# A planner with per-engine hand-over delays, TensorE's side work held back a set time behind its operands, and the residual multiplied by the norm's factor on VectorE instead of GpSimd

## The chip, the cores and the metric

One core of one Trainium2 chip runs the whole program. The metric is the time of one execution in device microseconds, the median of several runs. The engines are named as the profile names them: PE is TensorE's matrix multiply and PEld its weight load, DVE is VectorE, ACT is ScalarE, POOL is GpSimd, SP is SyncE, which here only starts transfers.

## The reference

Two layers, each with a mixer of three branches and a feed-forward block with a short convolution, over 272 positions (16 learned ones and 256 of the sequence) and 1024 features, in float32. The reference pads to 384 and masks; the rows that count are these 272.

```python
for li in range(DEPTH):
    h = h + mixer(rms_norm(h, norm_mix_g[li]), w_in[li], w_branch[li], w_out[li], ...)
    h = h + conv_ffn(rms_norm(h, norm_ffn_g[li]), w_ffn_in[li], ffn_conv_w[li], ...)
h = rms_norm(h, norm_final_g)

def mixer(hn, ...):
    rq, rk, rv, rg, hq, hf, hi, hg, dq, dk, dv, mg = jnp.split(hn @ w_in, offs, axis=-1)
    branches = [retention(rq, rk, rv, rg), hgrn2(hq, hf, hi, hg), diff_attention(dq, dk, dv)]
    y_b = jnp.einsum('blnc,ncd->blnd', branches, w_branch)
    return jnp.sum(jax.nn.sigmoid(mg) * y_b, axis=2) @ w_out

def conv_ffn(hn, ...):
    c = conv_b + sum(conv_w[j] * shifted(hn @ w_ffn_in, j) for j in range(3))
    gate, val = jnp.split(c, 2, axis=-1)
    return (silu(gate) * val) @ w_ffn_out
```

`rms_norm` divides each row by the root of its mean square and multiplies by a gain per feature. In `diff_attention` each head makes two softmaxes of scores and takes one minus lambda times the other.

## The kernel before

**Layout.** Features lie on the 128 partitions, positions run along the free dimension, so `h` is 8 tiles of 128x272 and every weight matrix is cut into 128x128 tiles. To keep float32 accuracy at the fast matmul rate, each weight tile and each activation tile is split into a rounded part and a rest (`whi`, `wlo`, `xh`, `xl`), and a product is three matmuls, lines 915 to 917: `xh` with `whi`, `xl` with `whi`, `xh` with `wlo`. These are the **main** products; 9,432 of the 10,594 matmuls in the program belong to them. In layer 1 most of them are 258 columns wide instead of 272. All other PE work (scores, transposes, sums over partitions, small products of the branches) is called **side work** here, and one unbroken run of it between main products a side block.

**Weights.** They come in chunks of 8 tiles (128x1024) through three buffers. For each chunk SP starts a transfer to `wraw`, ACT copies it to `whi` and DVE subtracts to give `wlo` (class `_Weights`, line 612). Each of `whi` and `wlo` has four buffers.

**Pairs.** The main products run in a fixed sequence, `ORDER`, of named pairs of output tiles, for instance `hq 0` or `fi 3`; `fi` are the 22 pairs of the feed-forward's first matrix. Each pair takes 8 tiles deep times 2, that is 48 main matmuls.

**The norm's factor.** At the start of the `w_in` products and of the `fi` products the factor `rstd` is not known yet. The first four pairs (`DEFER = 4`) therefore use `h` times the gain alone, and their results are multiplied by `rstd` when they leave PSUM (for `fi` into `two_a`). When the fifth pair begins, `Norm.next` (line 862) makes `y = h * rstd` for the eight tiles, and from `y` a new `xh` (ACT) and `xl` (DVE); from then on nothing has to be multiplied afterwards. This text calls the place a **fold**. There are four of them: before the fifth pair of `w_in` and of `fi` in both layers. Before the change POOL makes `y`, one 128x272 product after another.

After a `fi` pair, ACT and DVE do the convolution: ACT scales the last tap into `two_b`, DVE adds the other two taps with four SCALAR_TENSOR_TENSOR instructions, ACT applies SiLU, DVE multiplies gate and value (`two_b`), ACT and DVE split the result into `ghi` and `glo`.

**Attention heads.** A head group of `diff_attention` starts with the scores of the 16 learned positions of four heads at once: PE writes `ds`, DVE and ACT make the softmax in `wts`, and PE transposes it (`wt`). Then come the four heads, each: scores `ds` on PE, masked copies with row sums `two_a` and `two_b` on DVE, exponentials on ACT, the difference of the two softmaxes into `two_a` on DVE, three transposes `wt` on PE (line 1317), two products `do`, and a norm over partitions (`hsq` on ACT, `hr` on POOL). There are two such groups in each layer. Meanwhile DVE also rotates the next queries and keys: a shuffle into `two_c`, two multiplications and an addition into `dq` or `dk`.

**The order.** No line of the program says when side work runs. Every instruction is recorded with an engine, a cost in microseconds, a due time (`key`) and its dependencies. `_Plan.order` (line 454) then plays all engines in time and picks for each engine the instruction that can start first, and among those the one with the lowest rank, which is the due time with corrections. For PE's side work the correction is `HOLD` (later) or, next to other side work whose operands have been there for `SURE`, `PULL` (earlier). A result is taken to be usable on another engine `CROSS = 0.4` us after its end. The engines then execute their lists in that order, each list strictly in sequence, and wait on semaphores. `behind` records one step of a branch and chains it to earlier steps of the same branch.

Of the kernel before, what the change touches and what calls it, by code (L numbers as in the profile page):

```python
# [48 lines left out]
BACK = 0.09  # L49
# [299 lines left out]
class _Op:  # L349
    __slots__ = ("engine", "run", "cost", "key", "func", "tiles", "need", "after", "ready", "fed")  # L350

    def __init__(self, engine, run, cost, key, func):
        self.engine, self.run, self.cost, self.key, self.func = engine, run, cost, key, func
        self.tiles, self.need, self.after, self.ready, self.fed = set(), 0, [], 0.0, 0.0


class _Plan:
# [3 lines left out]
    CROSS = 0.4  # L361
    FREE = 0.5
# [64 lines left out]
    def queue(self, first, last):  # L427

        first.need += 1
        last.after.append(first)  # L430
# [23 lines left out]
    def order(self):  # L454
# [49 lines left out]
        while len(out) < todo:  # L504
# [35 lines left out]
            if e == "pe":  # L540
                if op in mains:
                    cost += BACK if beside else 0.0
# [31 lines left out]
class _Engine:  # L574
# [5 lines left out]
    def __getattr__(self, method):  # L580
        f = getattr(self.engine, method)

        def call(*args, **kw):
# [7 lines left out]
            elif self.name == "pool" and method != "memset":  # L591
                cost += 1.6e-3 * n
            if method == "partition_all_reduce":
                cost = 0.4 + 5.4e-3 * n
# [6 lines left out]
            elif method == "matmul" and args[1].dtype == F32R:  # L601
                cost = max(0.107, n / 2400 + 0.003)
            elif method == "matmul":
                cost = max(0.214 if args[1].shape[-1] > 32 else 0.07, 4 * n / 2400)
            elif method == "dma_start":
                cost = self.fixed + self.each * n * outs[0].shape[0]
# [60 lines left out]
def _trace(ctx, tc, plan, a, depth, probe):  # L667
    nc = tc.nc
    act = _Engine(plan, nc.scalar, "act", 0.094, 0.833e-3)
    dve = _Engine(plan, nc.vector, "dve", 0.068, 1.042e-3)  # L670
# [148 lines left out]
    class Norm:  # L819
# [42 lines left out]
        def next(self):  # L862
# [29 lines left out]
    def products(xs, name, j, t0=0):  # L892
# [12 lines left out]
        cost = 3 * ((T - t0) / 2400 + 0.003)  # L905
# [724 lines left out]
```

## Time and profile before

| what | value |
|---|---|
| median of 3 runs | 1301.27 us (1298.95 to 1302.18) |
| the profiled execution | 1298.69 us |
| its span, first to last instruction | 1296.9 us |
| DVE busy in the span | 74% |
| ACT busy in the span | 65% |
| POOL busy in the span | 13% |
| granted TensorE clock | 0.999 |

The page's first part gives busy time by engine; matmuls overlap in it, so a busy PE does not by itself mean that no time is lost. Lost time on PE shows better in the waits of PEld, the weight load: it stands in front of each matmul and waits for the same operands. Many rows carry line 607, because that one line issues every recorded instruction that is not a main product; there the tile names tell the rows apart.

### The profile page before, as it was taken

Reading aid. Unit: us, or ns where it says so; the run is one execution under the profiler, and the core shown is the slowest. Engines: PE = TensorE matmul, PEld = TensorE weight load, DVE = VectorE, ACT = ScalarE, POOL = GpSimd, SP = SyncE. Lnnn points to the kernel's source line nnn. Section 1 sums busy time; section 2 is a strip of 40 time slices with the busy share of each in tenths; the row PEclk is TensorE's granted clock in tenths of the full one; section 3 lists DMA queues with packets and bytes.
Section 4 is the critical chain, followed back from the end, with each engine's and each line's share of the span. In section 5 each row is a group of like instructions: output and inputs, shape, how many; then the busy total and the mean of one; then the engine's idle time right before and its main releaser. Section 6 shows DMA issues by size and latency. Waiting matters only on the chain.

```text
span 1296.9 us, 28609 instructions
## 1 busy us (share of the span) xinstructions
PE 1284.4 (99%) x11678; PEld 1255.9 (97%) x11678; DVE 960.9 (74%) x1589; ACT 838.6 (65%) x1376; POOL 166.8 (13%) x204
## 2 busy tenths in 40 slices
PE   9999999999999999999999999999999999999998
PEld 9999999999999999999999999999999999999986
DVE  7675787698585789886575767786985867898843
ACT  6766585856676567666457664858567765777643
POOL 4001111222121020000030011112220310200000
PEclk9999999999999999999999999999999999999999
DMA  7654574543644545555555645745546456366653
GB/s 269 205 164 160 170 205 142 160 161 125 201 145 155 183 154 178 181 178 179 179 172 186 192 151 172 214 140 170 170 131 198 145 169 204 134 210 195 203 189 112
DMA packets 86868, 225.36 MB, mean 174 GB/s; under 512 B 32976, under 2 KB 33104, under 8 KB 86736
## 3 DMA queue, kind: packets, MB, share of 16 engines
q1 hardware_dynamic: 86448, 223.00, 54.3%
q8 instruction: 92, 1.51, 0.5%
q10 hardware_dynamic: 288, 0.52, 0.1%
q14 instruction: 40, 0.33, 0.1%
HBM read 216.16 MB, written 1.05 MB: 167 GB/s over the span
## 4 chain that ended last, share of the span: by engine, by line
PE 91%; DVE 6%; issue 1%; ACT 1%; DMA 0%; SPq 0%; DVEq 0%
PE main L915 27%; PE main L917 26%; PE main L916 26%; PE fo L1430 2%; PE fo L1431 2%; PE fo L1429 2%; DVE wlo L607 1%; PE lev L1107 1%; DVE two_b L607 1%; DVE two_a L607 1%; PE ds L1291 1%; PE ro L607 1%; PE ho L607 1%; PE do L607 1%; DVE two_c L607 1%
## 5 line engine op out<-in xcount | busy, mean ns | idle before, releaser
L915 PE MATMUL main<-xh,whi 128*128 128x272 f32 (+1 forms) x2368 | 682.0, 288 | 0.0
L916 PE MATMUL main<-xl,whi 128*128 128x272 f32 (+1 forms) x2368 | 672.8, 284 | 1.5 <-DVE xl L607 1.5
L917 PE MATMUL main<-xh,wlo 128*128 128x272 f32 (+1 forms) x2368 | 673.3, 284 | 0.8 <-DVE wlo L607 0.5
L607 DVE TENSOR_TENSOR wlo<-wraw,whi 128x1024 fp32r<-128x1024 f32 (+1 forms) x411 | 502.7, 1229 | 192.2 <-ACT whi L607 185.5
L607 ACT ACTIVATE whi<-wraw 128x1024 fp32r<-128x1024 f32 (+1 forms) x411 | 426.5, 1041 | 229.6 <-PE main L916 145.7
L917 PEld LDWEIGHTS main<-xh,wlo 128*128 128x128 f32 x2368 | 445.9, 188 | 2.5 <-DVE wlo L607 2.4
L916 PEld LDWEIGHTS main<-xl,whi 128*128 128x128 f32 x2368 | 446.1, 188 | 2.2 <-DVE xl L607 1.9
L915 PEld LDWEIGHTS main<-xh,whi 128*128 128x128 f32 x2368 | 446.2, 188 | 1.4 <-ACT whi L607 0.2
L607 DVE SCALAR_TENSOR_TENSOR two_b<-main,small,two_b 128x256 f32<-128x256 f32 (+2 forms) x144 | 65.3, 487 | 25.0 <-ACT two_b L607 23.3
L607 POOL PARTITION_ALL_REDUCE hr<-hsq x36 | 67.2, 1877 | 114.7 <-ACT hsq L607 112.5
L607 POOL TENSOR_TENSOR y<-h,rstd 128x272 f32<-128x272 f32 x32 | 34.5, 1111 | 318.1 <-ACT rstd L607 318.1
L607 ACT ACTIVATE two_b<-main,small 128x272 f32<-128x272 f32 (+1 forms) x72 | 37.3, 566 | 25.1 <-PE main L917 24.0
L915 PE MATMUL main<-ghi,whi 128*128 128x272 f32 x176 | 51.0, 290 | 0.0
L916 PE MATMUL main<-glo,whi 128*128 128x272 f32 x176 | 50.6, 287 | 0.0
L917 PE MATMUL main<-ghi,wlo 128*128 128x272 f32 x176 | 50.3, 286 | 0.0
L607 POOL COPY tails<-vsrc 128x32 f32<-128x32 f32 x32 | 10.6, 344 | 224.4 <-ACT vsrc L607 223.0
L915 PE MATMUL main<-b0hi,whi 128*128 128x272 f32 (+1 forms) x128 | 37.9, 296 | 0.0
L915 PE MATMUL main<-b1hi,whi 128*128 128x272 f32 (+1 forms) x128 | 37.9, 296 | 0.0
L915 PE MATMUL main<-yhi,whi 128*128 128x272 f32 (+1 forms) x128 | 36.4, 284 | 0.0
L916 PE MATMUL main<-b0lo,whi 128*128 128x272 f32 (+1 forms) x128 | 36.4, 284 | 0.0
L917 PE MATMUL main<-yhi,wlo 128*128 128x272 f32 (+1 forms) x128 | 36.4, 284 | 0.0
L916 PE MATMUL main<-b1lo,whi 128*128 128x272 f32 (+1 forms) x128 | 36.3, 284 | 0.0
(235 smaller groups left out, 1938.6 us busy)
## 6 DMA issues: line engine op xcount, KB each, us to landing
wraw<-in_w SPq DMA_DIRECT2D x402, 512.0 KB, 3.5
h<-in_h SPq DMA_DIRECT2D x4, 272.0 KB, 5.7
dec<-in_dec SPq DMA_DIRECT2D x2, 544.0 KB, 6.9
wraw<-in_w SPq DMA_DIRECT2D x4, 256.0 KB, 4.6
const<-in_const SPq DMA_DIRECT2D x1, 937.0 KB, 7.6
turned<-apart SPq DMA_TRANSPOSE x48, 3.0
gain<-in_gl SPq DMA_DIRECT2D x1, 512.0 KB, 5.2
out<-y ACTq DMA_DIRECT2D x2, 256.0 KB, 2.8
```

The source lines that it names most:

```text
L607: self.plan.add(self.name, lambda: f(*args, **kw), cost, outs, ins, args[2] if method == "activation" else None)
L915: nc.tensor.matmul(o, wh, hi, start=first, stop=False)
L916: nc.tensor.matmul(o, wh, lo, start=False, stop=False)
L917: nc.tensor.matmul(o, wl, hi, start=False, stop=last)
L1107: nc.tensor.matmul(o, keys, x, start=True, stop=True)
L1291: nc.tensor.matmul(ss[m][:, at : at + nk], q[half, hd, q0 : q0 + P], k[half, hd, :nk], start=True, stop=True)
L1429: nc.tensor.matmul(o, gh, wh, start=False, stop=False)
L1430: nc.tensor.matmul(o, gl, wh, start=False, stop=False)
L1431: nc.tensor.matmul(o, gh, wl, start=False, stop=end)
```

## The change

1. `y = h * rstd` at the four folds moves from POOL to DVE. POOL made eight 128x272 products per fold; DVE makes two of 128x1088. The due times move from 12 us ahead of the fifth pair (0.3 us apart) to 9 us ahead (2.8 us apart).
2. The planner's hand-over times change. `CROSS = 0.4` becomes a table by producing engine, `LAG` (0.12 to 0.20 us, 2.0 us for transfers); a dependent instruction on the same engine gets a delay of its own (`SAME`); a buffer is free again `LAG + 0.05` after its last use instead of 0.5. Links that only set a sequence (`queue`) carry no delay any more.
3. Side work on PE is held back until 0.7 us after its last operand from another engine (`SAFE`). The 0.09 us that each return from side work to main products cost in the plan (`BACK`) is dropped.
4. The costs of many instructions are changed in the plan. A main product of three matmuls of 272 columns is planned with 0.3685 us instead of 0.349.
5. A step of a head of `diff_attention` may begin when the step two before it has reached its eighth last instruction, instead of its last.

```diff
-BACK = 0.09
+SAFE = 0.7
...
-    CROSS = 0.4
-    FREE = 0.5
+    LAG = {"pe": 0.20, "act": 0.13, "dve": 0.12, "pool": 0.15, "sp": 2.0}
+    SAME = {"pe": 0.0, "act": 0.13, "dve": 0.12, "pool": 0.1, "sp": 0.0}
+    FREE = 0.05
...
         first.need += 1
-        last.after.append(first)
+        last.then.append(first)
...
             if op.engine == "pe" and op not in mains:
+                if op.fed + SAFE > t:
+                    return math.inf
                 return op.key - PULL if beside and op.fed + SURE <= t else op.key + HOLD
...
             if e == "pe":
-                if op in mains:
-                    cost += BACK if beside else 0.0
                 beside = op not in mains
...
-            done = t + cost + (2.0 if e == "sp" else 0.0)
+            done = t + cost
...
-                    free[self.tag[n]].append(done + self.FREE)
+                    free[self.tag[n]].append(done + self.LAG[e] + self.FREE)
...
                 if o.engine != e:
-                    o.fed = max(o.fed, done + self.CROSS)
-                o.ready = max(o.ready, done + (self.CROSS if o.engine != e else 0.0))
+                    o.fed = max(o.fed, done + self.LAG[e])
+                o.ready = max(o.ready, done + (self.LAG if o.engine != e else self.SAME)[e])
+                if o.need == 0:
+                    push(o)
+            for o in op.then:
+                o.need -= 1
+                o.ready = max(o.ready, done)
...
-            elif method == "matmul" and args[1].dtype == F32R:
-                cost = max(0.107, n / 2400 + 0.003)
             elif method == "matmul":
-                cost = max(0.214 if args[1].shape[-1] > 32 else 0.07, 4 * n / 2400)
+                cost = max(0.218 if args[1].shape[-1] > 32 else 0.07, 4 * n / 2400 + 0.02)
...
-    act = _Engine(plan, nc.scalar, "act", 0.094, 0.833e-3)
-    dve = _Engine(plan, nc.vector, "dve", 0.068, 1.042e-3)
+    act = _Engine(plan, nc.scalar, "act", 0.105, 0.833e-3)
+    dve = _Engine(plan, nc.vector, "dve", 0.065, 1.052e-3)
...
-                plan.key = clock[0] - 12.0 + 0.3 * k
                 if k % 4 == 0:
+                    plan.key = clock[0] - 9.0 + 0.7 * k
                     ys.append(slot4("y"))
+                    tt(ys[-1], h[:, k : k + 4, :], pair(rstd, 4), MUL)
                 y = ys[-1][:, k % 4, :]
-                pool.tensor_tensor(out=y, in0=h[:, k, :], in1=rstd, op=MUL)
                 plan.key = clock[0] - 6.0 + 0.7 * k
...
-        cost = 3 * ((T - t0) / 2400 + 0.003)
+        cost = 3 * ((T - t0) / 2400 + 0.0095)
...
-        def behind(f, until, apart=1):
+        def behind(f, until, apart=1, after=1):
...
-            mine.append(ops)
+            mine.append((ops, after))
             if len(mine) > apart:
-                plan.queue(ops[0], mine[-1 - apart][-1])
+                before, which = mine[-1 - apart]
+                plan.queue(ops[0], before[-which])
...
-                    behind(lambda: da_head(b, hd), "da", 2)
+                    behind(lambda: da_head(b, hd), "da", 2, 8)
```

The instructions themselves stay the same but for `y`: 32 fewer on POOL, 8 more on DVE. Besides, POOL's list has 4 bare ISA rows without operands instead of 7, and ACT's list has 33 loads of function tables instead of 29. PE's list has the same 10,594 matmuls; its side work stands in 123 blocks instead of 129. Three places show what moves.

First, DVE in layer 0, where the softmax of the learned positions (`wts`) is made for the transpose `wt` that PE waits for; `two_c` and `dq` are the rotation of the next queries, `wlo` is a weight chunk. Before:

```order
L607 TENSOR_TENSOR wlo_640<-wraw_638,whi_639 128x4x256
L607 RECIPROCAL wts_556<-wts_556 128x1
L607 TENSOR_TENSOR wts_556<-wts_556,fmap_85 128x1
L607 TENSOR_REDUCE wts_556<-wts_556 128x16
L607 STREAM_SHUFFLE two_c_628<-main_621 128x544
L607 TENSOR_TENSOR dq_310_619<-main_621,const_79 128x544
L607 TENSOR_TENSOR two_c_628<-two_c_628,const_79 128x544
L607 TENSOR_TENSOR dq_310_619<-dq_310_619,two_c_628 128x544
L607 TENSOR_SCALAR wts_556<-wts_556 128x16
```

and now:

```order
L619 TENSOR_TENSOR wlo_635<-wraw_633,whi_634 128x4x256
L619 RECIPROCAL wts_556<-wts_556 128x1
L619 TENSOR_REDUCE wts_556<-wts_556 128x16
L619 TENSOR_TENSOR wts_556<-wts_556,fmap_85 128x1
L619 TENSOR_SCALAR wts_556<-wts_556 128x16
L619 TENSOR_TENSOR wlo_640<-wraw_638,whi_639 128x4x256
L619 STREAM_SHUFFLE two_c_628<-main_621 128x544
L619 TENSOR_TENSOR dq_310_619<-main_621,const_79 128x544
```

The four rows of the rotation and one weight chunk have moved from in front of the last `wts` instruction to behind it.

Second, DVE at the fourth head of layer 0's first group: the softmax difference into `two_a`, for which PE's three transposes wait. `dk` is the rotation of the next keys, `y` here a gated sum of the branches. Before:

```order
L607 TENSOR_SCALAR dm_597<-dm_597 128x4
L607 TENSOR_TENSOR wlo_679<-wraw_677,whi_678 128x1024
L607 STREAM_SHUFFLE two_c_667<-main_659 128x544
L607 TENSOR_TENSOR dk_321_666<-main_659,const_79 128x544
L607 RECIPROCAL dm_597<-dm_597 128x4
L607 TENSOR_TENSOR dm_597<-dm_597,nlam_97 128x2
L607 TENSOR_SCALAR two_b_594<-two_b_594,dm_597 128x272
L607 SCALAR_TENSOR_TENSOR two_a_593<-two_a_593,dm_597,two_b_594 128x272
L607 TENSOR_SCALAR two_b_594<-two_b_594,dm_597 128x144
L607 SCALAR_TENSOR_TENSOR two_a_593<-two_a_593,dm_597,two_b_594 128x144
```

and now:

```order
L619 TENSOR_TENSOR wlo_671<-wraw_669,whi_670 128x1024
L619 TENSOR_SCALAR dm_597<-dm_597 128x4
L619 TENSOR_TENSOR y_318_651<-main_652,m_213_474 128x544
L619 RECIPROCAL dm_597<-dm_597 128x4
L619 TENSOR_TENSOR dm_597<-dm_597,nlam_97 128x2
L619 TENSOR_SCALAR two_b_594<-two_b_594,dm_597 128x272
L619 TENSOR_SCALAR two_b_594<-two_b_594,dm_597 128x144
L619 SCALAR_TENSOR_TENSOR two_a_593<-two_a_593,dm_597,two_b_594 128x272
L619 SCALAR_TENSOR_TENSOR two_a_593<-two_a_593,dm_597,two_b_594 128x144
```

The shuffle and the first product of the rotation no longer stand between the row sums and `two_a`; one product of `y` does.

Third, DVE at the `fi` fold of layer 1, in the four pairs ahead of it (`xl_17` is the new split rest for the first four tiles, `xl_15` for the last four). Before:

```order
L607 TENSOR_TENSOR wlo_2018<-wraw_2016,whi_2017 128x1024
L607 SCALAR_TENSOR_TENSOR two_b_1996<-two_a_1995,small_76,two_b_1996 128x256 x4
L607 TENSOR_TENSOR two_a_2004<-main_1997,rstd_93 128x2x258
L607 TENSOR_TENSOR wlo_2021<-wraw_2019,whi_2020 128x1024
L607 SCALAR_TENSOR_TENSOR xl_17_92<-y_2024,small_76,xh_16_91 128x272 x2
L607 TENSOR_TENSOR two_b_1996<-two_b_1996 128x256
L607 SCALAR_TENSOR_TENSOR two_b_2005<-two_a_2004,small_76,two_b_2005 128x256 x4
L607 TENSOR_TENSOR two_a_2013<-main_2006,rstd_93 128x2x258
L607 TENSOR_TENSOR glo_1994<-two_b_1996,ghi_1993 128x256
L607 TENSOR_TENSOR two_b_2005<-two_b_2005 128x256
L607 TENSOR_TENSOR wlo_2029<-wraw_2027,whi_2028 128x1024
```

and now, from the second of the two `y` on:

```order
L619 TENSOR_TENSOR y_2025<-h_78,rstd_93 128x1088
L619 TENSOR_TENSOR glo_1994<-two_b_2005,ghi_1993 128x256
L619 SCALAR_TENSOR_TENSOR two_b_2014<-two_a_2013,small_76,two_b_2014 128x256 x4
L619 TENSOR_TENSOR wlo_2029<-wraw_2027,whi_2028 128x1024
L619 TENSOR_TENSOR two_b_2014<-two_b_2014 128x256
L619 SCALAR_TENSOR_TENSOR xl_17_92<-y_2024,small_76,xh_16_91 128x272 x2
L619 TENSOR_TENSOR glo_1994<-two_b_2014,ghi_1993 128x256
L619 SCALAR_TENSOR_TENSOR xl_17_92<-y_2024,small_76,xh_16_91 128x272 x2
L619 SCALAR_TENSOR_TENSOR xl_15_90<-y_2025,small_76,xh_14_89 128x272
L619 TENSOR_TENSOR wlo_2032<-wraw_2030,whi_2031 128x1024
L619 SCALAR_TENSOR_TENSOR xl_15_90<-y_2025,small_76,xh_14_89 128x272 x3
```

The first `xl_17` stood ahead of the convolution of the second pair and now stands behind that of the third; the chunk `wlo_2032`, which stood ahead of all `xl_15`, now stands behind the first of them. The fold of layer 0's `fi` is rearranged in the same way.

More of the change, by code (lines that the diff above doesn't have):

```diff
@@ L590, in call @@
                 cost += 0.093 * (len(aps) - 2) - (0.043 if ins[0].tensor.name in self.plan.psum else 0.0)
[L591 to L594, printed above, removed]
+                if outs[0].dtype == U16 and outs[0].ap[-1][0] == 2:
+                    cost += 0.33e-3 * n
+            elif method == "tensor_scalar":
+                cost += 0.065 * (len(aps) - 2) - 0.14
+            elif method in ("scalar_tensor_tensor", "stream_shuffle", "tensor_tensor_reduce"):
+                cost += 0.06
+            elif self.name == "pool" and method == "tensor_tensor":
+                cost = 0.55 + 2.1e-3 * n
+            elif self.name == "pool" and method == "tensor_copy":
+                cost = 0.2 + 1.0e-3 * n
+            elif method == "partition_all_reduce":
+                cost = 0.2 + 6.3e-3 * n
             if method == "reciprocal":
```

8 lines of the change are left out of this document (4 added, 4 removed).

## The prediction

> **What bounds the kernel now.** First the page: span, busy time, and the chain that ended last.
>
> ```profile
> span 1296.9 us, 28609 instructions
> PE 1284.4 (99%) x11678; PEld 1255.9 (97%) x11678; DVE 960.9 (74%) x1589; ACT 838.6 (65%) x1376; POOL 166.8 (13%) x204
> PE 91%; DVE 6%; issue 1%; ACT 1%; DMA 0%; SPq 0%; DVEq 0%
> ```
>
> PE sets the end nearly everywhere. The change removes no matmul, so what it can win is only what PE loses: waits for operands, and the price of going from main products to side work and back. The waits show in the weight load, which stands in front of each matmul.
>
> ```profile
> PEld wt L1317 <- DVE two_a L607: 2.7, 5, 0.7
> PEld main L917 <- DVE wlo L607: 2.4, 8, 0.5
> PEld main L916 <- DVE xl L607: 1.9, 2, 1.3
> PEld wt L607 <- issue: 1.9, 2, 1.2
> ```
>
> The columns are the sum in us, the number of waits, the longest. So 2.7 and 1.9 us go to the attention's transposes `wt`, and 4.3 us to main products that wait for a weight rest or a new `xl`. The four rows together are 8.9 us, 0.7% of the span. That is the ceiling for the waits; there is no such ceiling for a loss.
>
> The 4.3 us lie mostly at the `fi` folds. Two windows, one for each layer, show who is full there (columns: busy time and instructions of PE, PEld, DVE, ACT, POOL; clock; DMA):
>
> ```profile
> 472.00:504.00 32.00, 31.24 (x249) 30.59 (x248) 31.03 (x52) 23.23 (x41) 8.11 (x8) 1.00 0.39 129
> 1112.00:1144.00 32.00, 30.73 (x257) 29.98 (x256) 31.49 (x54) 23.89 (x43) 8.62 (x8) 1.00 0.44 145
> ```
>
> DVE is busy 31.03 and 31.49 of 32 us against 74% on average. There DVE is the bound, and the change puts work on it.
>
> **The change part by part.** *The two `wt` that wait for `wts`.* One of them, in layer 0:
>
> ```profile
> 281.32 0.41 PE L607 MATMUL wt<-const,wts 128*128 128x64 f32 x2 [1.05 <-DVE wts L607]
> 281.53 0.37 PE L915 MATMUL main<-b0hi,whi 128*128 128x272 f32 x1
> 281.74 0.28 PE L916 MATMUL main<-b0lo,whi 128*128 128x272 f32 x1
> ...
> 277.81 0.16 DVE L607 RECIPROCAL wts<-wts 128x1 f32<-128x1 f32 x1
> 278.08 0.25 DVE L607 TENSOR_REDUCE wts<-wts 128x16 f32<-128x64 f32 x1
> 278.26 0.78 DVE L607 STREAM_SHUFFLE two_c<-main 128x544 f32<-128x544 f32 x1
> 280.30 0.72 DVE L607 TENSOR_TENSOR dq<-dq,two_c 128x544 f32<-128x544 f32 x1
> 280.94 0.23 DVE L607 TENSOR_SCALAR wts<-wts 128x16 f32<-128x16 f32 x1
> ```
>
> The last `wts` step could start when the reduction ends, at 278.33, but the rotation stands in front of it until 280.94. In the new order it follows at once, 2.6 us earlier, more than the longest wait of 1.2. The order has PE at the same place in layer 0 (66 main matmuls behind the scores, before and now); in layer 1 PE comes 9 matmuls earlier there, some 1.1 us at 0.12 each, and the same four rows have left, so 1.5 us of cover remain for a wait of 0.7. Both waits go: **-1.9 us**.
>
> *The `wt` behind `two_a`.* The order gives the number of main matmuls between a head's scores and its transposes, before and now, at the five that wait: 57 to 75, 57 to 60, 60 to 54, 57 to 63, 63 to 66. The second of them on DVE:
>
> ```profile
> 314.98 0.78 DVE L607 STREAM_SHUFFLE two_c<-main 128x544 f32<-128x544 f32 x1
> 315.66 0.70 DVE L607 TENSOR_TENSOR dk<-main,const 128x544 f32<-128x544 f32 x1
> 317.07 1.34 DVE L607 SCALAR_TENSOR_TENSOR two_a<-two_a,dm,two_b 128x272 f32<-128x272 f32 x1
> 318.94 0.37 DVE L607 SCALAR_TENSOR_TENSOR two_a<-two_a,dm,two_b 128x144 f32<-128x144 f32 x1
> ```
>
> There the shuffle and the `dk` product (0.68 and 0.62 from start to start) leave the list and one product of `y`, of `dk`'s size, comes in: 0.7 us earlier, and PE 3 matmuls or 0.4 us later, 1.1 against a wait of at most 0.7. The first has 18 matmuls (2.2 us) more, the fourth 6 (0.7 us) and a shorter list. These three go. The third has PE 0.7 us earlier, and the fifth has a list grown by a product of the next head; I leave both their waits. At the mean of 2.7/5, three are **-1.6 us**; the bounds are -2.7 (all go) and +1 (the third doubles and another head's `wt` begins to wait).
>
> *`y` at the `fi` folds.* What POOL's `y` costs DVE is seen in the same kinds of DVE instruction beside it and after it:
>
> ```profile
> 1112.23 8.62 POOL L607 TENSOR_TENSOR y<-h,rstd 128x272 f32<-128x272 f32 x8 [61.92 <-ACT rstd L607]
> ...
> 1113.21 1.62 DVE L607 TENSOR_TENSOR wlo<-wraw,whi 128x1024 fp32r<-128x1024 f32 x1 [0.33 <-ACT whi L607]
> 1114.75 3.74 DVE L607 SCALAR_TENSOR_TENSOR two_b<-two_a,small,two_b 128x256 f32<-128x256 f32 x4
> 1120.15 1.43 DVE L607 SCALAR_TENSOR_TENSOR xl<-y,small,xh 128x272 fp32r<-128x272 f32 x2
> 1121.83 1.66 DVE L607 SCALAR_TENSOR_TENSOR two_b<-two_a,small,two_b 128x256 f32<-128x256 f32 x4
> 1128.57 1.22 DVE L607 TENSOR_TENSOR wlo<-wraw,whi 128x1024 fp32r<-128x1024 f32 x1
> 1129.70 0.90 DVE L607 SCALAR_TENSOR_TENSOR xl<-y,small,xh 128x272 fp32r<-128x272 f32 x2
> 1130.53 0.41 DVE L607 TENSOR_TENSOR two_b<-two_b 128x256 f32<-128x256 f32 x1
> ...
> 474.90 1.78 DVE L607 TENSOR_TENSOR wlo<-wraw,whi 128x1024 fp32r<-128x1024 f32 x1 [0.67 <-ACT whi L607]
> 476.61 3.80 DVE L607 SCALAR_TENSOR_TENSOR two_b<-two_a,small,two_b 128x271 f32<-128x271 f32 x4
> 483.28 1.98 DVE L607 SCALAR_TENSOR_TENSOR two_b<-two_a,small,two_b 128x271 f32<-128x271 f32 x4
> ...
> 1128.71 0.28 PE L917 MATMUL main<-xh,wlo 128*128 128x258 f32 x1
> 1128.83 0.28 PE L915 MATMUL main<-xh,whi 128*128 128x258 f32 x1
> 1130.25 0.39 PE L916 MATMUL main<-xl,whi 128*128 128x258 f32 x1 [1.14 <-DVE xl L607]
> ...
> L607 DVE TENSOR_TENSOR b1lo<-hg,b1hi 128x1088 fp32r<-128x1088 f32 x2 | 2.5, 1286 | 0.0
> ```
>
> In layer 1 POOL's eight products cost DVE 0.40 on the chunk (1.62 to 1.22), 2.08 on four taps (3.74 to 1.66) and 0.53 on two `xl` (1.43 to 0.90): 3.0 us. In layer 0 it is 0.56 (1.78 to 1.22) and 1.82 (3.80 to 1.98): 2.4; one more slowed chunk there is moved ahead of the wait for `rstd` and counts for nothing. What DVE takes over has the size of `b1lo`: two of 1.29 us, less the 0.09 by which a next instruction starts early (1128.57 to 1129.70 is 1.13 for a duration of 1.22), 2.4 us a fold. So DVE gains 0.6 in layer 1 and nothing in layer 0: **-0.6 us**. The bounds: none of the relief comes and PE pays 2.4 twice, +4.8; or all the waits there go except the restarts, -3.
>
> The end of DVE's full stretch decides, but PE's wait moves forward in it. In layer 1 `wlo_2032` (1128.57 to 1129.79 before) gets 2.4 of `y` ahead of it, one `xl`, one `two_b`, one `glo` (0.41, 0.33, 0.33 from start to start) and loses 3.0: it ends at 1130.3. The first new `xl` stands five `xl`, a `glo` and that chunk ahead of this, so it ends near 1127.1. PE's fifth pair begins 24 matmuls of 0.12 before 1128.83, at 1126.0. So PE should wait about 1.1 us at the pair's first `xl` where it waited 1.14 at the fifth, and little behind it.
>
> The Trainium skill (Perfetto Trace Analysis, Optimizing Scalar/DVE Operations) speaks against this part: when DVE is saturated, moving work to GpSimd may pay, and here work comes back. It adds that the two share a read port, so that moving between them might not help. The 3.74 against 1.66 is with the second half; by the first half alone the sum would be 1302.1, which is the first rival below.
>
> *The two `w_in` folds.* PE loses nothing there now, and DVE has gaps; I put 0, -0.2 to +2.4.
>
> *Side blocks,* 129 to 123. After a block the second main matmul starts 0.21 us behind the first (281.53 to 281.74) where 0.12 is usual, and by the kind of block the way in can cost as much again: 0.09 each for six blocks, **-0.5 us**, between 0 and -1.1.
>
> *Everything else the new delays move.* ACT gets four more table loads; one took
>
> ```profile
> 1115.99 1.28 ACT L607 ACT_TABLE_LOAD   x1
> ```
>
> so 5.1 us on an engine that is 35% idle. They are hidden behind that idle time; one that stands in front of a needed `whi` in a fold would cost its 1.28. Neither SP's queue nor a transfer is moved past anything that PE waits for. Side work held back 0.7 us makes its users on DVE and ACT wait, and behind these stand `wlo` and `whi`; outside the folds none of the rows of PEld's waits names them beyond the start of the program, so there is room. I add nothing.
>
> **Sum.** -1.9 - 1.6 - 0.6 - 0.5 = -4.6 us. The profiled execution took 1298.69 (the span and 1.8 around it), so 1294.1 for such a one; it lies 2.6 under the median of the runs shown, 1301.27, so the median comes to **1296.7 us**, 0.35% less.
>
> **The rivals.**
>
> *`y` lands on PE's path.* The relief is eaten by new DVE waits for ACT, since the new order puts more rows that need ACT's results (`two_b`, `glo`) in front of the first `xl`. Then the folds cost +4.8 instead of -0.6: 1296.7 + 0.6 + 4.8 = 1302.1. For it: DVE is full there, and 1127.1 against 1126.0 leaves it no slack. Against: POOL's cost to DVE is measured beside its cause. Chance 0.14.
>
> *The planner's delays only shift the waits.* The two `wts` waits go, the five `two_a` waits stay or change places, the folds lose 1 us: -1.9 - 0.5 + 1 = -1.4, 1299.9. For it: two of the five look no better in the order. Chance 0.17. Here the change would not do what its delays say.
>
> *Slower.* At both `fi` folds PE's fifth pair waits for its first `xl` while DVE idles: three rounds of taps, SiLU and split, each with a hand-over between DVE and ACT ahead of that `xl`. If each costs DVE the 1.1 us that the plain sum has PE waiting already, it is 3.3 a fold on top of 1.1: 8.8 in place of the present 4.3, and with the heads' waits kept (-1.9 - 0.5) the sum is +2.1; for slower by 0.3% (+3.9) DVE must idle some 4.2 us a fold, or a table load stand in that chain as well, twice 1.28, which gives +4.7 and 1306.0. For it: ACT's SiLU in a fold waits for a table load now too. Against: ACT has a quarter of the window free. Chance 0.15.
>
> **How the numbers follow.** The forecast has 0.54, the rivals 0.14, 0.17 and 0.15. About 0.3%, 3.9 us, is what a measurement of this kernel can tell from no change: under 1297.4 is faster, over 1305.2 slower. The forecast lies 0.7 us inside faster with bounds on both sides, so I count 0.50 of it there, and 0.04 as the same. Faster 0.51 (with a little of the second rival), same 0.33, slower 0.16. Range: down to 1292 (all waits of the heads go, the folds win 2) and up to 1304 (the first rival and 2 us of scatter); 1306 is left out.
>
> **What would show it.** PEld's row for `wt` behind `wts` should be gone, that behind `two_a` near 1 us with two waits. DVE's chunk and taps behind `rstd` in the `fi` folds should show 1.2 and 1.7 to 2.0 us, `y` two rows of 1.29. PE's wait in layer 1 should be at the first `xl` of the fifth pair, near 1 us, and the row of `main` behind `wlo` and `xl` together near 4. DVE's total should stay near 960, POOL's fall by about 34. It would be wrong if DVE shows idle time in the folds, if main products wait for `wlo` or `whi` in the middle of a head group, or if PEld names operands that it did not wait for before.

## The result, and the profile after

The changed kernel takes 1303.93 us (median of 20 runs, 1300.62 to 1307.98) beside 1300.57 for the kernel before (20 runs, 1298.3 to 1303.5). The ratio is 1.0024, 95% interval 1.0016 to 1.0032. The prediction was 1296.7 and faster; by the medians the kernel became 3.4 us slower. That is less than the 3.9 us that the prediction took as the least that can be told from no change, but the interval excludes no change, and the direction is the opposite of the forecast. The profiled execution took 1301.13 us, 2.4 more than that of before, and the 2.4 us stand in its span as well.

The page of the changed kernel, its span and busy time:

```profile
span 1299.3 us, 28554 instructions
PE 1284.0 (99%) x11678; PEld 1255.5 (97%) x11678; DVE 938.6 (72%) x1597; ACT 838.2 (65%) x1380; POOL 143.7 (11%) x172
```

PE is as busy as before (1284.0 us against 1284.4), so all that changed is what PE loses. DVE has 22 us less although `y` came to it, but little of that comes from `y`: with `y` alone on DVE, a run shown below, its total is 957.4 against 960.9, and with `y` back on POOL in the changed kernel it is 940.2. So the new order makes most of the 22 us; which of its edits does was not tested. POOL fell by 23 us, not by the 34 of its `y`, because its `dt` copies grew by 12 (from 12.9 to 24.8). The waits of the weight load (sum in us, number, longest; `issue` means that the profile shows nothing it waited for):

```profile
PEld wt L619 <- POOL dt L619: 4.3, 4, 2.2
PEld main L929 <- DVE wlo L619: 2.1, 6, 0.4
PEld main L928 <- DVE xl L619: 1.7, 2, 1.4
PEld ho L619 <- issue: 1.3, 2, 0.7
PEld main L929 <- issue: 1.1, 1, 1.1
PEld do L619 <- PE main L929: 0.8, 1, 0.8
```

The rows of `wt` behind `two_a` and `wts` (2.7 and 1.9 us before) are gone. The two rows of main products behind `wlo` and `xl` sum to 3.8 instead of 4.3; without the waits at the program's start, the `fi` folds themselves have 3.0 instead of 3.4. In place of the waits that are gone stands a row that the kernel before did not have at all: `wt` waits for POOL's `dt`, 4.3 us, and smaller ones for `ho` and `do`. `dt` is a copy of 16 columns. The view of that one tile, first of before, then of the changed kernel (minimum, median, maximum in ns):

```profile
L607 POOL COPY dt<-two_a x32: 193/198/1131, 290.0 to 1038.0; 128x16 f32<-128x16 f32 x32
```

```profile
L619 POOL COPY dt<-two_a x32: 189/266/3677, 290.2 to 1039.9; 128x16 f32<-128x16 f32 x32
```

A copy that takes 0.19 us at its shortest takes up to 3.68. The end of the last head in layer 0 shows why; the timeline of the changed kernel, PE, POOL and DVE one after the other (start, duration, what ended the idle time before):

```profile
387.67 0.49 PE L1329 MATMUL wt<-const,two_a 128*128 128x128 f32 x3
390.08 0.33 PE L619 MATMUL wt<-const,dt 128*128 128x128 f32 x1 [1.92 <-POOL dt L619]
...
387.35 2.68 POOL L619 COPY dt<-two_a 128x16 f32<-128x16 f32 x2 [2.67 <-DVE two_a L619]
...
386.79 0.77 DVE L619 SCALAR_TENSOR_TENSOR two_a<-two_a,dm,two_b 128x272 f32<-128x272 f32 x2
387.48 2.35 DVE L619 TENSOR_TENSOR wlo<-wraw,whi 128x1024 fp32r<-128x1024 f32 x2
```

The row of POOL holds two copies. The first begins at 387.35, while DVE works on the last `two_a`; DVE begins two `wlo` back to back at 387.48, and the copy ends only behind the second of them (389.83), after 2.55 us. The second copy takes 0.19 and ends at 390.03. PE stands for 1.92 us. Layer 1 has the same picture 650 us later (two chunks of `wlo` from 1037.57, PE idle 1.42). The ten long copies of `dt` in this trace all look like that: they last 1.13 to 1.41, 2.54 to 2.55 or 3.68 us, and each ends just behind one, two or three chunks. In the plan the copy costs 0.22 us, its hand-over 0.15 and the hold 0.7; none of them can cover 2.5.

The two waits for `ho` come from the same two engines with the roles exchanged. Layer 0:

```profile
258.00 3.96 POOL L619 PARTITION_ALL_REDUCE hr<-hsq  x2 [5.97 <-ACT hsq L619]
...
260.12 2.20 DVE L619 TENSOR_TENSOR wlo<-wraw,whi 128x1024 fp32r<-128x1024 f32 x1
262.24 0.71 DVE L619 TENSOR_TENSOR dk<-dk,two_c 128x544 f32<-128x544 f32 x1
262.88 0.43 DVE L619 TENSOR_TENSOR ho<-ho,hr 128x272 f32<-128x272 f32 x1
...
263.45 0.46 PE L619 MATMUL ho<-at,vt 128*128 128x128 f32 x2 [0.50 <-DVE ho L619]
```

Here POOL has begun first: its second all-reduce starts near 259.8, DVE's chunk 0.3 us behind it, and the chunk takes 2.20 instead of 1.22. (In the kernel before, the chunk nearest to this place, at 260.65, starts 1.8 us behind an all-reduce and takes 1.21.) The product that frees `ho`'s bank stands two places behind, 1 us late, and PE waits.

### The profile page after: what moved, and what is told of

It reads as the page before. It is cut to its first block, busy times and chain, and to the rows that moved or that the text cites. A ratio compares the mean times of both kernels' runs of the same rounds, so it can differ in the third digit from the quotient of the medians.

```text
span 1299.3 us, 28554 instructions
## 1 busy us (share of the span) xinstructions
PE 1284.0 (99%) x11678; PEld 1255.5 (97%) x11678; DVE 938.6 (72%) x1597; ACT 838.2 (65%) x1380; POOL 143.7 (11%) x172
## 3 DMA queue, kind: packets, MB, share of 16 engines
HBM read 216.16 MB, written 1.05 MB: 167 GB/s over the span
## 4 chain that ended last, share of the span: by engine, by line
PE 88%; DVE 7%; issue 1%; ACT 1%; POOL 1%; DMA 0%; SPq 0%; DVEq 0%
PE main L927 26%; PE main L929 26%; PE main L928 26%; DVE wlo L619 2%; DVE two_b L619 2%; PE fo L1442 2%; PE fo L1444 2%; PE fo L1443 2%; PE lev L1119 1%; PE ho L619 1%; PE ro L619 1%; PE ds L1303 1%; DVE two_a L619 1%; DVE y L619 1%; DVE xl L619 1%
## 5 line engine op out<-in xcount | busy, mean ns | idle before, releaser
L619 DVE SCALAR_TENSOR_TENSOR two_b<-main,small,two_b 128x256 f32<-128x256 f32 (+2 forms) x144 | 61.1, 485 | 29.1 <-ACT two_b L619 29.1
L929 PE MATMUL main<-b0hi,wlo 128*128 128x272 f32 (+1 forms) x128 | 36.4, 284 | 0.0
```

The lines of the kernel that those rows point to most:

```text
L619: self.plan.add(self.name, lambda: f(*args, **kw), cost, outs, ins, args[2] if method == "activation" else None)
L929: nc.tensor.matmul(o, wl, hi, start=False, stop=last)
```

## The experiments

Ratios are against the kernel before, timed on the same chip, with 95% intervals. Where an experiment's edit leaves the order of PE untouched (`dt` on ACT, both runs on `y`, the shorter all-reduce), a difference cannot come from another place of the side work.

**`dt` copied by ACT.** In the changed kernel:

```diff
-                pool.tensor_copy(st[f"dt{b}"][:, g, hd, :], w[:, c : c + TAIL])
+                plan.add("pool", lambda to=st[f"dt{b}"][:, g, hd, :], src=w[:, c : c + TAIL]: nc.scalar.activation(to, src, AF.Copy), 0.2 + 1.0e-3 * TAIL, [st[f"dt{b}"][:, g, hd, :]], [w[:, c : c + TAIL]])
```

> The changed kernel, with the 32 copies of 16 columns that fill `dt` issued by ACT at the places of the plan where POOL issued them; the orders of PE, DVE and SP are word for word those of the changed kernel. Theory (POOL's copies of 0.2 us stand still while DVE runs chunk after chunk of `wlo`; the plan allowed 0.7 us for the hand-over): PE's row `wt` behind `dt`, 4.3 us in the changed kernel (two long waits, 1.96 and 1.46 us between matmul starts), falls under 0.3, and the time falls by 3.0 to 3.4 us against the changed kernel, to about the time of the kernel before (1300.5). Rival (the two `wt` would wait there anyway, because the order put PE too close behind the last head's `two_a`): the row names ACT or DVE instead of POOL with 1 us or more left, and the time falls by less than 1.5 us.

Measured: 1299.75 us, ratio 0.9999 (0.999 to 1.0008), so 0.0025 or 3.2 us under the changed kernel. The row of `wt` behind `dt` is gone. The same place, ACT, PE and DVE:

```profile
388.33 0.31 ACT L1336 ACTIVATE dt<-two_a 128x16 f32<-128x16 f32 x2
...
388.71 0.31 PE L619 MATMUL wt<-const,dt 128*128 128x128 f32 x1
...
388.21 2.35 DVE L619 TENSOR_TENSOR wlo<-wraw,whi 128x1024 fp32r<-128x1024 f32 x2
```

DVE runs the same two chunks at the same place, ACT's two copies take 0.31 us beside them, and PE goes on without a wait. The theory holds; the rival falls. Between the two profiles the stretches of PE's work that hold the heads (their bounds are given below) differ by 2.6 us, less than the 3.2 by the ratios. PE also comes earlier to `do` now, whose waits grow from 0.8 to 1.9 us. That alone brings the change back to the time of before, not under it.

**`y` back on POOL, and `y` alone on DVE.** Once in the changed kernel, with the products `y` and their due times as before; once in the kernel before, with those of the change:

```diff
+                plan.key = clock[0] - 12.0 + 0.3 * k
                 if k % 4 == 0:
-                    plan.key = clock[0] - 9.0 + 0.7 * k
                     ys.append(slot4("y"))
-                    tt(ys[-1], h[:, k : k + 4, :], pair(rstd, 4), MUL)
                 y = ys[-1][:, k % 4, :]
+                pool.tensor_tensor(out=y, in0=h[:, k, :], in1=rstd, op=MUL)
```

> The changed kernel with the products `y` back on POOL, 32 of 272 columns with their old due times; PE's order is nearly that of the changed kernel. My prediction's term (DVE gains 0.6 us by having `y`): slower than the changed kernel by 0.3 to 1 us, with the waits for `xl` and `wlo` at the two `fi` folds at 3.8 us again instead of 3.5. Rival (`y` on DVE costs PE time somewhere): faster than the changed kernel by 1 us or more. The two waits of `wt` behind `dt` stay in both.

> The kernel before with `y` on DVE as the only edit, the old planner kept; PE's order is that of the kernel before, word for word. Prediction's term: 0.3 to 1 us faster than before; the waits of `wt` behind `wts` and `two_a` stay at 1.9 and 2.7 us. Rival (`y` lands on PE's path): slower by 2 to 5 us, with the waits for `xl` and `wlo` at the `fi` folds above 5 us together.

Measured: `y` back on POOL 1308.19 us, ratio 1.0068 (1.0055 to 1.0082), 5.7 us slower than the changed kernel, far more than my 0.3 to 1. `y` alone 1298.88, ratio 0.9995 (0.9986 to 1.0003), 0.7 us, as forecast, though the interval holds no change. The rows of the `fi` folds do not bear out the 0.6 us as they should: `y` alone takes their waits from 3.4 to 1.3 us, and `y` back on POOL, where I expected more waiting, has 2.6 against the changed kernel's 3.0. The surplus of the first run is at the `w_in` fold of layer 0, where I had put nothing: PE with `y` on POOL in the changed order.

```profile
34.80 0.39 PE L928 MATMUL main<-xl,whi 128*128 128x272 f32 x1 [0.60 <-DVE xl L619]
37.60 0.59 PE L928 MATMUL main<-xl,whi 128*128 128x272 f32 x1 [1.78 <-DVE xl L619]
39.78 0.59 PE L928 MATMUL main<-xl,whi 128*128 128x272 f32 x1 [0.45 <-DVE xl L619]
```

These waits of PE are 2.8 us. About as much again comes behind them, where PE works at half its rate. The window from 40 to 44 us, first this run, then the changed kernel (PE's matmuls are the first count, the granted clock is the third number from the end):

```profile
40.00:44.00 4.00, 4.00 (x18) 4.00 (x19) 1.77 (x3) 1.68 (x2) 0.00 (x0) 0.50 0.40 138
40.00:44.00 4.00, 4.00 (x34) 4.00 (x34) 2.43 (x2) 2.38 (x4) 0.00 (x0) 1.00 0.67 212
```

With a granted clock of 0.50 the main matmuls start 0.23 us apart instead of 0.12, some 26 of them from 37.6 us on, which makes 2.7 us by my estimate. All five executions of this run have a mean granted clock of 0.995 to 0.997, against 0.999 in the profile of the changed kernel. So the 5.7 us are not the price of the late `xl` alone; The profile of `y` alone has such a place too: a wait of 1.6 us at 839 us, and a granted clock of 0.50 from 841 to 843. But the wait of 1.9 us for `dt` in the changed kernel has none behind it, so what brings the clock down stays open here.

POOL's first `y` comes later there, first the kernel before, then this run:

```profile
21.81 7.75 POOL L607 TENSOR_TENSOR y<-h,rstd 128x272 f32<-128x272 f32 x7 [2.65 <-ACT rstd L607]
```

```profile
24.46 4.89 POOL L619 TENSOR_TENSOR y<-h,rstd 128x272 f32<-128x272 f32 x5 [5.66 <-ACT rstd L619]
```

POOL begins 2.6 us later because `rstd` does; in the changed kernel itself `rstd` is 2.0 us later than before (it ends at 23.75 instead of 21.73), and DVE's two quick products make up for that. So the move of `y` is no part of the loss; the rest of the change needs it.

**Without the overlap of the heads.**

```diff
-                    behind(lambda: da_head(b, hd), "da", 2, 8)
+                    behind(lambda: da_head(b, hd), "da", 2)
```

> The changed kernel without the overlap of the attention's heads: each head begins again only when the one two before it is done. Theory (POOL's copies stand still behind DVE's chunks; the place of the chunks in the order decides): `wt` behind `dt` still waits wherever two chunks stand behind the last head's `two_a`, and the `two_a` waits stay away because PE's side work is held back 0.7 us behind its operands; the time stays within 2 us of the changed kernel. Rival (the overlap packs the heads so that DVE and POOL come late): the `dt` waits go and the time falls by 2.5 us or more.

Measured: 1298.17 us, ratio 0.9981 (0.9969 to 0.9992), 5.6 us under the changed kernel. The numbers of the rival came: the `dt` waits are gone, and the `two_a` waits stay away. But POOL's copies are still slow (20.0 us in 32 copies, against 24.8 in the changed kernel and 12.9 before), and one of 1.41 us stands near the end of each layer's heads; PE has merely other work between it and the transpose. So the lock makes `dt` late, and the overlap makes it matter. I counted the time that PE takes from its 1800th to its 3000th main matmul and from its 6600th to its 7800th, the two stretches with the attention's heads: 337.65 us before, 339.43 changed, 336.83 with `dt` on ACT, 335.24 without the overlap. Of the overlap's 4.2 us, 2.6 are `dt`. The other 1.6 are mostly `do`, which waits until its bank has been read. The row of PE's own waits in the run with `dt` on ACT, and its timeline of POOL and DVE in layer 0:

```profile
PE do L619 <- DVE da L619: 1.3, 3, 0.6
```

```profile
390.10 2.12 POOL L619 PARTITION_ALL_REDUCE hr<-hsq  x1 [9.54 <-ACT hsq L619]
...
390.69 1.92 DVE L619 TENSOR_TENSOR wlo<-wraw,whi 128x1024 fp32r<-128x1024 f32 x1
393.25 0.49 DVE L619 SCALAR_TENSOR_TENSOR da<-do,subg,hr 128x256 f32<-128x256 f32 x1 [0.65 <-ACT hr L619]
```

Again a chunk that starts within an all-reduce (1.92 us) stands ahead of `da`; here `da` then waits 0.65 us more for `hr`, which needs the same all-reduce.

**A shorter all-reduce.** On the run without overlap, in `ho`'s inverse norm. This kernel leaves out the sum over the partitions for all but 16 of the 272 columns, so that POOL's instruction becomes short:

```diff
-                inverse(r[:, t0:], sq[:, t0:], P)
+                _short(plan, nc, act, eps, r[:, t0:], sq[:, t0:])
...
+    plan.add("pool", lambda: nc.gpsimd.partition_all_reduce(r[:, :16], sq[:, :16], P, ReduceOp.add), 0.2 + 6.3e-3 * n, [r], [sq])
+    plan.add("act", lambda: nc.scalar.activation(r, sq, AF.Ln, bias=eps, scale=1.0 / P), cost + 0.093, [r], [r, eps], AF.Ln)
```

> The changed kernel without the overlap of the heads, and with the all-reduce of `ho`'s squares over 16 of its 272 columns on POOL (the sum over the partitions is left out for the rest; ACT goes on from the squares); the orders of PE, DVE and SP are those of the run without overlap word for word. Theory (POOL's all-reduce holds the port that DVE's chunk needs: 2.1 to 2.2 us for a chunk of 1.22 that starts 0.3 to 0.6 us behind it, and the chunk stands ahead of the product that frees `ho`): the chunks at 260 and 907 us take 1.2 us, and the two waits of `ho`, 1.3 us together, fall under 0.3; time 1 to 1.5 us under the run without overlap. Rival (`ho` waits for the chain of its own norm or for its place in DVE's queue): the chunks get shorter but the waits stay above 0.8.

Measured: 1296.55 us, ratio 0.9961 (0.9949 to 0.9973). That is 0.0020 or 2.6 us under the run without overlap, with intervals that touch; the heads' stretches of the profile fall from 335.24 to 333.97 us, by 1.3, within the 1 to 1.5 that the theory forecast; the other half of the 2.6 was not traced. DVE at the place of `ho` in layer 0:

```profile
259.46 1.22 DVE L619 TENSOR_TENSOR wlo<-wraw,whi 128x1024 fp32r<-128x1024 f32 x1
260.60 0.72 DVE L619 TENSOR_TENSOR dk<-dk,two_c 128x544 f32<-128x544 f32 x1
261.76 0.44 DVE L619 TENSOR_TENSOR ho<-ho,hr 128x272 f32<-128x272 f32 x1 [0.44 <-ACT hr L619]
```

The chunk is back at 1.22, as is that of layer 1 (at 904.80); the waits of `ho` fall from 1.3 us to one of 0.2. The orders of PE and DVE are the same. The shorter all-reduce also brings `hr` earlier, but in the run without overlap DVE's `ho` product starts right behind `dk`, without a wait for `hr`. So it was the chunk, held up by the all-reduce, that delayed `ho`.

**The hold alone, and the change without it.** In the kernel before, and in the changed kernel:

```diff
             if op.engine == "pe" and op not in mains:
+                if op.fed + 0.45 > t:
+                    return math.inf
```

```diff
-SAFE = 0.7
+SAFE = 0.0
```

> The kernel before with one edit: side work of PE may not start until 0.45 us after the planner's time for its operands, which has a hand-over of 0.4 in it (0.85 together, as much as hand-over and hold in the changed kernel). Theory (the hold does it): the waits of `wt` for `wts` (1.9 us) and `two_a` (2.7) shrink by 3 us or more, time 2 to 4 us below before, unless a new wait shows. Rival (the measured costs are needed for it): the rows stay above 3 us together.

> The changed kernel with the 0.7 us by which TensorE's side work is held behind its operands set to 0; the other edits kept. Theory (the hold took the waits of `wt` for `wts` and `two_a` away): waits of side work for its operands come back, in PE's rows for side work 4 us or more beside those that the changed kernel has now, and the waits behind `dt` grow (0.7 us less between the copy and the transpose); time 3 us or more above the changed kernel's 2.4 over before. Rival (the new costs and delays did it, the hold adds nothing): the rows of `wt` behind `wts` and `two_a` stay gone and the time stays within 1.5 us of the changed kernel.

Measured: the hold alone 1298.01 us, ratio 0.9976 (0.9964 to 0.9988); the change without it 1304.31, ratio 1.002 (1.001 to 1.0031). The hold alone takes `two_a` away and leaves 0.7 of 1.9 us of `wts`:

```profile
PEld wt L609 <- issue: 0.7, 2, 0.5
```

Its rows and its time, 3.1 us under before, are as its theory says. That one edit is worth as much as the whole change without the overlap (0.9976 against 0.9981, and 335.23 us in the heads' stretches against 335.24): nothing shows that the new costs, the new delays and `y` on DVE add to it. In the change without the hold these rows stand:

```profile
PEld wt L1329 <- DVE two_a L619: 3.3, 5, 0.8
PEld wt L619 <- POOL dt L619: 2.2, 3, 1.1
PEld lev L1119 <- issue: 2.2, 7, 0.7
```

`two_a` is back, so the hold removes it; `wts` is not, so that was the order on DVE. The time was the rival's, though: it did not move. The waits behind `dt` shrank from 4.3 to 2.2 us instead of growing, and those at the `fi` fold of layer 0 nearly vanished (1.0 to 0.3). Which of these is the hold's and which the other order's was not taken apart.

**A planner that knows of the lock.** The run without overlap, `dt` copied by DVE, and in the planner, where `took` holds the end of DVE's last two-input operation and the stretch in which POOL holds the port (from 0.4 us after an all-reduce begins, by the durations above; `port` marks DVE's two-input operations and POOL's, and the lines that set it are not shown):

```diff
+            if op.port == "dve":
+                if took[1] <= t < took[2]:
+                    cost += took[2] - t
+                took[0] = t + cost
+            elif op.port:
+                first = 0.4 if op.port == "all" else 0.0
+                cost += max(0.0, took[0] - t - first)
+                took[1:] = t + cost - op.cost + first, t + cost - (0.3 if first else 0.0)
```

> The changed kernel without the overlap of the heads, with `dt` copied by DVE, and with a planner that knows of the lock: a DVE operation with two inputs in SBUF that would start while POOL holds the port ends later by the rest, and a POOL operation that starts while DVE has such an operation running ends later by the rest. Theory (what is left of the heads' waits comes from the lock): the waits of `ho` and of `wt` behind `dt` are gone, and the time is 1 to 2.5 us below the run without overlap (1298.2), 0.25% to 0.4% below before. Rival (another order, other accidents): waits of the same size at other places, time within 1 us of the run without overlap or above it.

> The run with the planner that knows of the lock once more, as the neighbour of the other runs here and for a second profile: 0.9955 to 0.9975 of before. Theory that single stalls of 1 to 1.7 us at a few places (PE at 180 us for a chunk of `wlo`, the first chunk at 5 us) vary from one execution to the next and belong to no order: the one at 181 us is of another size in this profile.

Measured: 1297.45 us, ratio 0.9964 (0.9952 to 0.9976), and in a second series 1296.75, ratio 0.997 (0.9959 to 0.9981). It is faster than both kernels, by 0.30% to 0.36% than before; from the hold alone (0.9976) its intervals do not tell it apart. The waits of the second profile:

```profile
PEld main L943 <- DVE wlo L628: 2.4, 7, 0.4
PEld main L942 <- DVE xl L628: 2.3, 3, 1.4
PEld main L941 <- ACT whi L628: 0.7, 1, 0.7
PEld main L943 <- issue: 0.5, 1, 0.5
PEld ho L628 <- issue: 0.3, 1, 0.3
PEld ho L628 <- DVE ho L628: 0.3, 1, 0.3
```

No `wt` or `do` is left, `ho` is at 0.6, and the stretches of the heads take 333.80 us. Against the run without overlap the gain is 0.0011 to 0.0017, near what the theory forecast, but with overlapping intervals, so that the time does not show what the planner's lock is worth; the rows of `ho` fell from 1.5 us in all to 0.6. The same program's first profile has the row `issue` with 1.4 us in one wait at 181 us where this one has 0.5. The changed kernel has 1.1 us there, and the run without overlap and the run with `dt` on ACT, whose orders are the same up to that place, none. Such a wait belongs to the execution, not to the change.

**Three neighbours of it.** The same planner with the overlap; with `LEAD = 8.0` instead of 6.0 (load and split of a chunk due earlier); with `SAFE = 0.4`.

> As the run with the planner that knows of the lock and `dt` copied by DVE, but with the overlap of the heads as in the changed kernel. Theory (the overlap costs only because it puts the tails of the heads where POOL and DVE meet, and the planner didn't know): with the lock planned and the copies off POOL it is within 1 us of the run with that planner and no overlap, near 0.9965 of before. Rival (the overlap packs DVE and ACT so that transposes and `do` come late in any case): PE waits of `do` and `wt` of 2 us or more in sum remain, and the time is 2 to 3 us above that run, near 0.9985 of before.

> The same planner, with each chunk's load and split due 8 us ahead of its products instead of 6. Theory (what is left of PE's waits, some 4 us at the two `fi` folds and 1 to 2 us at single chunks, comes from DVE and ACT being full there): 1 us or less of gain or loss. Rival (the chunks are simply due too late): 1.5 us faster or more, with the row of main products behind `wlo` cut from 2.8 us to under 1.5.

> The same planner, with the hold 0.4 us instead of 0.7. Theory (with the lock planned, the planner's times are good enough that a shorter hold covers the rest): within 1 us of the run with 0.7, no `wt` row above 0.5 us. Rival (the hold covers more than the lock): the `wt` rows behind `two_a` come back with 1 us or more, and the time rises by 1 to 2 us.

Measured: with the overlap 1298.54 us, ratio 0.9989 (0.998 to 0.9998); the shorter hold 1296.61, 0.9975 (0.9963 to 0.9986); the earlier chunks 1301.36, 1.0011 (1.0003 to 1.002). The overlap no longer costs `dt` (`wt` and `do` wait 0.7 us together, and the heads' stretches take 334.52, 0.7 more than without it), so the rows are its theory's. The time is nearer the rival's: the medians are 1.8 us apart, the ratios 0.0019. Where the rest lies was not found. The shorter hold is the same within the interval and has no `wt` row, as its theory says. Earlier chunks are the worst of the three, which neither side expected: the row behind `wlo` does fall, to 0.6 us, but DVE's `xl` is pushed back, as its waits show.

```profile
PEld main L942 <- DVE xl L628: 6.3, 8, 1.4
```

## Why the prediction was wrong

1303.93 us lies just inside the range of 1292 to 1304, and that is luck: its upper end was set for `y` on PE's path and scatter, and `y` did not land there.

**The waits for `wts`: right.** -1.9 us forecast, and the row is gone. It stays gone without the hold, as the working by the order on DVE said.

**The waits for `two_a`: right in kind, too small.** I took three of five away for -1.6; all five went, -2.7. The hold alone does it. Where I counted on a shorter list of DVE I gave the wrong reason: with all the other edits and no hold, five waits of `two_a` stand, 3.3 us.

**`y` at the `fi` folds: the rows right, the share of `y` not shown.** The chunk and the four taps behind `rstd` in layer 1 of the changed kernel, with `y`:

```profile
1115.56 1.23 DVE L619 TENSOR_TENSOR wlo<-wraw,whi 128x1024 fp32r<-128x1024 f32 x1 [0.86 <-ACT whi L619]
1116.70 1.67 DVE L619 SCALAR_TENSOR_TENSOR two_b<-two_a,small,two_b 128x256 f32<-128x256 f32 x4
1118.89 1.28 DVE L619 TENSOR_TENSOR y<-h,rstd 128x1088 f32<-128x1088 f32 x1
...
1129.82 0.39 PE L928 MATMUL main<-xl,whi 128*128 128x258 f32 x1 [1.16 <-DVE xl L619]
```

1.23, 1.67 and 1.28 us, where 1.2, 1.7 to 2.0 and 1.29 were forecast, and PE's wait is at the fifth pair's first `xl`, 1.16 us by PE's idle time for a forecast of 1.1. The two rows of main products sum to 3.8 us for a forecast near 4. But the forecast's -0.6 comes out of neither run that moves `y` alone: to DVE in the old order, the folds' waits fall by 2.1 us; back to POOL in the new order, they fall again, by 0.4. DVE's total did not stay near 960; the 22 us are the order's, as the run with `y` back on POOL shows (940.2).

**The `w_in` folds: the sum right, the reason wrong.** PE still loses little there, but not because nothing happened: the rest of the change brought `rstd` 2.0 us later, and `y` on DVE paid for it.

**The step that failed** is the last one of the working, "Everything else the new delays move", with its "there is room" and "I add nothing". I looked for waits on ACT's table loads and on `wlo` and `whi` outside the folds, and took the hold of 0.7 us for cover enough on every hand-over. The overlap of the heads, the fifth edit, has no term of its own in the sum, and it is what turns the sign: without it the change is 5.6 us faster than with it, and 0.19% faster than before. I had measured in the folds that POOL slows DVE, and did not turn the row around: DVE stops POOL as well, here for up to three chunks. The new order puts the last head's `dt` in front of two chunks and PE's transpose right behind it, which cost 3.2 us by the run with `dt` on ACT, and the chunks in front of `ho` and `da` into POOL's all-reduces, some 2 us more by the rows of `ho` and `do`. -1.9 - 2.7 - 0.5 at the folds makes -5.1; with 4.3 for `dt`, 1.3 for `ho` and 0.8 for `do` the rows sum to +1.3, and with the 1.1 us at 181 us, which varies, to +2.4. The small rows left out (`whi` +0.4, `ds` +0.6, `lev` -0.4) make it +3.0, for a span that is 2.4 us longer. My -0.5 for six fewer side blocks is not told apart from that.

**The rivals.** The second, that the delays only shift waits, was nearest in its mechanism but not in its price (1299.9): the old waits did all go, and new ones of 6.4 us came at operands that no row of before named. The first, `y` on PE's path, has the price nearest to the result (1302.1), by chance. It and the third, hand-overs at the `fi` folds, are both contradicted by `y` back on POOL and by the fold's rows. The sign to look for that I had written down came true as it stood: "PEld names operands that it did not wait for before".

## What to carry to other kernels

A planner with a measured time for each operation alone still errs where two engines exclude each other: a POOL copy of 0.2 us took as long as three of DVE's chunks here, and the margin of 0.7 us did not cover that. Put such copies on ACT or DVE when PE waits for what they make; in the run with a planner that knows of the lock, the waits for `ho` fell as well. And where a change has several edits, run each alone: one line, the hold, gave 0.24%, and another, the overlap, took away 0.43%. Before counting a removed wait as gain, go through every engine that the new order places directly ahead of PE, including those that are hardly busy: POOL was 11% busy here and held PE up.

## What the runs showed of the hardware

POOL's copies and DVE's work with two inputs hold each other up. In the two profiles of before and after, 28 copies (`dt`, `wts`, `da`, `tails`) take between 1.05 and 3.96 us, where the shortest of their kinds take 0.19 to 0.24, and every one of them ends 0.05 to 0.11 us behind the end of a DVE instruction with two inputs. Where DVE goes straight on with a next chunk the outcome differs. Five `dt` copies of the changed kernel that had begun during the `two_a` product ahead of the chunks came through only behind the second or third chunk. Three copies that had begun within a chunk (at 313.59, 326.42 and 973.84 us) ended with it, though the next chunk had already begun 0.1 to 0.2 us before. The Trainium skill ("SBUF — State Buffer", Who interferes with whom) states that a DVE instruction with two SBUF inputs contends with a GpSimd instruction that reads SBUF, and that the port pair which the two share is an exclusive lock. The trace agrees, with 0.19 us becoming 3.68 on POOL and 1.22 becoming 2.20 on DVE.

I had not expected that an all-reduce holds DVE up only for a part of its time. In the profiles of before, after, `dt` on ACT and the run without overlap, a chunk that starts 0.3 to 0.6 us behind an all-reduce takes 1.85 to 2.2 us (once 1.6), one that starts 0.64 to 0.68 behind it 1.5 to 1.7, and one from 1.05 us on mostly 1.2, though the reduction still has 0.7 us to run. ACT's copies beside the same chunks took 0.31 us for two.
